# Row means of a 64 MiB tensor: other part sizes, larger load buffers, 12 loads of data in place of 14

## The chip, the core and the metric

The kernel runs on one core of one Trainium2 chip. The time is that of one execution on the device in microseconds (us): a median of 160.5 us over three runs, from 160.44 to 160.51. The profile shows one further execution of the same program, with the start and length of each instruction and of each packet of the DMA engines, which move data between the chip's main memory (HBM) and the core's own memory (SBUF).

## What is computed

```python
def setup_inputs():
    batch, seq, dim = 32, 512, 1024
    return {"x": np.random.randn(batch, seq, dim).astype(np.float32), "divisor": float(dim)}

def reference(x, divisor):
    return (np.sum(x, axis=-1) / divisor).astype(np.float32)
```

There are 32 x 512 = 16384 rows of 1024 floats, and each row becomes one number. The input is 64 MiB, read once; the output is 64 KiB. With 128 partitions each partition has J = 128 rows of 4 KiB.

## The kernel before

**Parts.** The rows are cut in three parts. The first part gives F rows to each partition, the main part M, the last part L, with F + M + L = 128 (L147 to L149). In HBM the first part is a block of its own at the front of x: partition p has rows p x F to p x F + F - 1, so that two partitions' rows lie F x 4 KiB apart (L150). Behind it each partition has W = M + L rows in one piece, the main part's first, and the distance between partitions is W x 4 KiB (L151, L152). The output has the same three parts (L153 to L155). Before, F = L = 16, M = 96, W = 112.

**Loads.** The lists `first`, `main` and `last` (L158 to L160) name the loads: a pair (rows, on_act) is one DMA that brings so many rows to every partition, and of these rows the last on_act are summed by ScalarE (ACT in the profile), the others by VectorE (DVE). All DMAs are issued by SyncE (SP) and stand in its one queue, which 16 DMA engines work off in the order of issue; `keep_in_program_order` (L182) holds that order to the order of the text. There are 12 loads into tiles `t`, and two of half a row each (`pa`, `pb`, L219 and L220) for the last row: 14 loads of data.

**Buffers.** The loads of `first` and `main`, and those of `last` with more than 4 rows, take turns in three buffers of 14 rows (pool `bulk`, L166 and L200); the loads of 4 and 2 rows have tiles of their own (`t4`, `t2`). A load into a bulk buffer waits on SP until the sums of the load three before it are done. Everything that stands behind it in SP's order waits with it.

**Sums.** In the first and main part one `reduce_sum` (L205) of VectorE sums all of a load's rows but ScalarE's; ScalarE sums a row with one ACTIVATE (L186). When a part is through, GpSimd (POOL) multiplies its sums by 1/1024 (L207). In the last part VectorE sums each row by an instruction of its own, which adds the row's two halves and scales at once (`dve_mean`, L192), and ScalarE scales as it sums. The last row comes as two halves: the sum of `pa` is put behind the elements of `pb`, and one last `dve_mean` over `pb` closes it (L226, L227).

**Stores.** The first part's means are stored by the DMA of L223, the main part's by L224, both behind all loads in SP's order, and the last part's by L228 after the last sum.

**The order by hand.** Three functions change the finished program. `start_loads_at_once` moves those loads that stand ahead of SP's first wait to the very start of the program: the first three. `latest_wait_first` sorts the waits of an instruction. `close_while_storing` lets the last store run beside the program's closing steps. The change leaves all three alone.

Of the kernel before, what the change touches and what calls it, by code (L numbers as in the profile page):

```python
# [9 lines left out]
F32 = mybir.dt.float32  # L10
# [115 lines left out]
@with_exitstack  # L126
def kernel(
    ctx: ExitStack,
    tc: tile.TileContext,
    x: bass.AP,  # L130
    divisor: float,
    out: bass.AP,
):
    nc = tc.nc
    landed = nc.alloc_semaphore("landed")
    nc.at_finalize(start_loads_at_once)
    nc.at_finalize(latest_wait_first)
    nc.at_finalize(lambda nc: close_while_storing(nc, landed))
    xf = x.flatten_outer_dims()
    N, D = xf.shape  # L140
    P = nc.NUM_PARTITIONS
    scale = 1.0 / float(divisor)
    J = N // P
    assert J * P == N


    F, L = 16, 16  # L147
    M = J - F - L
    W = M + L  # L149
    x_first = bass.AP(tensor=x.tensor, offset=0, ap=[[F * D, P], [D, F], [1, D]])  # L150
    x_main = bass.AP(tensor=x.tensor, offset=P * F * D, ap=[[W * D, P], [D, M], [1, D]])  # L151
    x_last = bass.AP(tensor=x.tensor, offset=P * F * D + M * D, ap=[[W * D, P], [D, L], [1, D]])  # L152
    o_first = bass.AP(tensor=out.tensor, offset=0, ap=[[F, P], [1, F]])  # L153
    o_main = bass.AP(tensor=out.tensor, offset=P * F, ap=[[W, P], [1, M]])
    o_last = bass.AP(tensor=out.tensor, offset=P * F + M, ap=[[W, P], [1, L]])  # L155


    first = [(2, 0), (14, 0)]  # L158
    main = [(14, 0)] * 5 + [(14, 4), (12, 5)]
    last = [(9, 4), (4, 2), (2, 1)]  # L160
    assert sum(n for n, _ in first) == F
    assert sum(n for n, _ in main) == M and sum(n for n, _ in last) == L - 1

    pad = ctx.enter_context(tc.tile_pool(name="pad", bufs=1))
    pad.tile([P, 224], F32, name="pad")
    bulk = ctx.enter_context(tc.tile_pool(name="bulk", bufs=3))  # L166
    one = ctx.enter_context(tc.tile_pool(name="one", bufs=1))
    psum = ctx.enter_context(tc.tile_pool(name="junk", bufs=4, space=bass.MemoryType.PSUM))


    c = 512
    t4 = one.tile([P, 4, D], F32, name="t4")
    t2 = one.tile([P, 2, D], F32, name="t2")
    pa = one.tile([P, 768], F32, name="pa")[:, :c]
    pb = one.tile([P, D - c + 16], F32, name="pb")[:, : D - c + 2]
    res0 = one.tile([P, F], F32, name="res0")
    res = one.tile([P, M], F32, name="res")
    fin = one.tile([P, L], F32, name="fin")
    nc.gpsimd.memset(pb[:, D - c :], 0.0)  # L179

    def load(dst, src):
        tc.keep_in_program_order(nc.sync.dma_start(out=dst, in_=src))  # L182

    def act_sum(dst, src, by=1.0):
        junk = psum.tile([P, D], F32, name="junk")
        nc.scalar.activation(junk, src, COPY, scale=by, accum_out=dst)  # L186

    def dve_mean(dst, src, by=scale):


        h = src.shape[-1] // 2
        nc.vector.tensor_tensor_reduce(  # L192
            out=src[:, :h], in0=src[:, :h], in1=src[:, h:], scale=by, scalar=0.0,
            op0=ADD, op1=ADD, accum_out=dst,
        )

    for loads, src, dst in ((first, x_first, res0), (main, x_main, res)):
        j = 0
        for rows, on_act in loads:
            t = bulk.tile([P, 14, D], F32, name="t")  # L200
            load(t[:, :rows, :], src[:, j : j + rows, :])
            d = rows - on_act
            for i in range(d, rows):
                act_sum(dst[:, j + i : j + i + 1], t[:, i, :])
            nc.vector.reduce_sum(out=dst[:, j : j + d], in_=t[:, :d, :], axis=AX)  # L205
            j += rows
        nc.gpsimd.tensor_scalar_mul(out=dst, in0=dst, scalar1=scale)  # L207
    j = 0
    for rows, on_act in last:
        t = bulk.tile([P, 14, D], F32, name="t")[:, :rows, :] if rows > 4 else t4 if rows == 4 else t2  # L210
        load(t, x_last[:, j : j + rows, :])
        d = rows - on_act
        for i in range(rows):
            if i < d:
                dve_mean(fin[:, j + i : j + i + 1], t[:, i, :])
            else:
                act_sum(fin[:, j + i : j + i + 1], t[:, i, :], by=scale)
        j += rows
    load(pa, x_last[:, j, :c])  # L219
    load(pb[:, : D - c], x_last[:, j, c:])  # L220


    tc.keep_in_program_order(nc.sync.dma_start(out=o_first, in_=res0))  # L223
    tc.keep_in_program_order(nc.sync.dma_start(out=o_main, in_=res))  # L224

    dve_mean(pb[:, D - c : D - c + 1], pa, by=1.0)  # L226
    dve_mean(fin[:, j:], pb)  # L227
    tc.keep_in_program_order(nc.sync.dma_start(out=o_last, in_=fin))  # L228
# [35 lines left out]
```

## Time and profile before

| what | value |
|---|---|
| median of 3 runs | 160.5 us (160.44 to 160.51) |
| span of the profiled execution, first to last instruction | 159.0 us |
| own time of the profiled execution, start and end included | not given; the runs' median lies 1.5 us above the span |
| VectorE busy | 117.2 us, 29 instructions |
| ScalarE busy | 18.5 us, 33 instructions |
| GpSimd busy | 1.0 us, 7 instructions |
| packets of SP's queue | 2448, 67.18 MB |
| bytes moved over the span, mean | 422 GB/s |
| VectorE idle ahead of L205, waiting for loads | 34.0 us in 9 times |
| SP waiting for L205 before it issues a load | 92.8 us in 7 times, 15.1 at most |
| SP waiting for GpSimd before the store of L224 | 21.6 us, once |

How to read it: a line of the timeline has the start in us, the length in us, the engine, the line of the program, the operation, what it writes and reads, and in square brackets how long the engine was idle before it and what ended that. A line of the groups by form has the same names, then the count, and after the bar the busy time in us, the mean length of one instruction in ns, and the idle time before. A line of the DMA issues ends with the size and the time from issue to landing, in which waiting in the queue is included. The row of GB/s has the bytes moved in each of 40 equal slices of the span, some 4 us each. The chain of work that ended last is followed backwards from the last instruction, at each step to what released it.

### The profile page before, as it was taken

How to read it: one execution, taken by the hardware profiler on the slowest of the kernel's cores; microseconds unless marked ns; L12 is line 12 of the kernel's file. 1: busy time of each engine (PE TensorE's matmuls, PEld its weight loads, DVE VectorE, ACT ScalarE, POOL GpSimd, SP SyncE). 2: the span in 40 equal slices, each digit the busy share in tenths (PEclk: the TensorE clock that was granted, in tenths of full speed). 3: DMA queues.
4: the chain of work that ended last, by engine and by line, in shares of the span. 5: the costliest groups of instructions: out<-in, count | busy, mean ns of one | idle time of the engine just before them, and what ended most of it. 6: DMA issues, size and time to landing. Idle time of an engine off the chain costs nothing.

```text
span 159.0 us, 148 instructions
## 1 busy us (share of the span) xinstructions
DVE 117.2 (74%) x29; ACT 18.5 (12%) x33; POOL 1.0 (1%) x7
## 2 busy tenths in 40 slices
DVE  0500059995999599978999599959995996395643
ACT  3000000000000000000000000000000900390684
POOL 0000000000000000000000000000000000001000
DMA  7999999959999999699999999699999999999894
GB/s 278 447 462 462 462 462 462 462 260 433 462 462 462 462 462 462 303 390 462 462 462 462 462 462 404 303 447 462 462 462 429 396 396 408 482 445 445 350 420 169
DMA packets 2448, 67.18 MB, mean 422 GB/s; under 512 B 656, under 2 KB 656, under 8 KB 912
## 3 DMA queue, kind: packets, MB, share of 16 engines
q1 hardware_dynamic: 2448, 67.18, 98.3%
HBM read 67.11 MB, written 0.07 MB: 422 GB/s over the span
## 4 chain that ended last, share of the span: by engine, by line
DMA 77%; DVE 21%; SPq 1%; issue 0%; DVEq 0%
DMA t<-in_x_dram 56%; DMA pb<-in_x_dram 21%; DVE res L205 20%; SPq L182 1%; DVE pb L192 0%; DVEq L259 0%
## 5 line engine op out<-in xcount | busy, mean ns | idle before, releaser
L205 DVE TENSOR_REDUCE res<-t 128x14 f32<-128x14336 f32 (+3 forms) x9 | 111.2, 12360 | 34.0 <-DMA t<-in_x_dram 34.0
L186 ACT ACTIVATE junk<-t 128x1024 f32<-128x1024 f32 x16 | 16.2, 1013 | 136.8 <-DMA t<-in_x_dram 136.8
L192 DVE CUSTOM_DVE_ANT_0 t<-t 128x512 f32<-128x512 f32 x8 | 5.1, 688 | 6.1 <-DMA t<-in_x_dram 6.1
L186 ACT ACTIVATION_READ_ACCUMULATOR junk<-t 128x1 f32 x16 | 3.0, 186 | 0.0
L207 POOL TENSOR_SCALAR res<-res 128x16 f32<-128x16 f32 (+1 forms) x2 | 0.7, 352 | 143.3 <-DVE res L205 143.3
L186 ACT ACT_TABLE_LOAD x1 | 1.3, 1283 | 1.7 <-PEq L245 1.7
L192 DVE DVE_READ_ACCUMULATOR2_ANT fin<- 128x1 f32 x9 | 0.7, 82 | 0.0
L192 DVE CUSTOM_DVE_ANT_0 pb<-pb 128x257 f32<-128x257 f32 x1 | 0.4, 428 | 0.2 <-DMA pb<-in_x_dram 0.2
L192 DVE CUSTOM_DVE_ANT_0 pa<-pa 128x256 f32<-128x256 f32 x1 | 0.4, 426 | 0.0
L179 POOL MEMSET pb<- 128x2 f32 x1 | 0.1, 99 | 1.3 <-POOLq L245 1.3
L245 POOL MEMSET const-bfloat16-1.0<- 128x1 bf16 x1 | 0.1, 101 | 0.0
L245 POOL MEMSET const-uint8-127<- 128x1 uint8 x1 | 0.1, 101 | 0.0
L245 POOL MEMSET const-float32-0.0<- 128x1 f32 x1 | 0.1, 98 | 0.2 <-issue 0.2
L245 POOL MEMSET const-float32-1.0<- 128x1 f32 x1 | 0.1, 98 | 0.0
L192 DVE DVE_READ_ACCUMULATOR2_ANT pb<- 128x1 f32 x1 | 0.1, 84 | 0.0
## 6 DMA issues: line engine op xcount, KB each, us to landing
t<-in_x_dram SPq DMA_DIRECT2D x7, 7168.0 KB, 35.6
t<-in_x_dram SPq DMA_DIRECT2D x1, 6144.0 KB, 33.3
t<-in_x_dram SPq DMA_DIRECT2D x1, 4608.0 KB, 27.2
t<-in_x_dram SPq DMA_DIRECT2D x2, 1024.0 KB, 19.2
t<-in_x_dram SPq DMA_DIRECT2D x1, 2048.0 KB, 31.7
pa<-in_x_dram SPq DMA_DIRECT2D x1, 256.0 KB, 33.8
pb<-in_x_dram SPq DMA_DIRECT2D x1, 256.0 KB, 33.9
out_dram<-res SPq DMA_DIRECT2D x1, 48.0 KB, 11.6
```

Source lines behind the costliest of these rows:

```text
L179: nc.gpsimd.memset(pb[:, D - c :], 0.0)
L182: tc.keep_in_program_order(nc.sync.dma_start(out=dst, in_=src))
L186: nc.scalar.activation(junk, src, COPY, scale=by, accum_out=dst)
L192: nc.vector.tensor_tensor_reduce(out=src[:, :h], in0=src[:, :h], in1=src[:, h:], scale=by, scalar=0.0, op0=ADD, op1=ADD, accum_out=dst,)
L205: nc.vector.reduce_sum(out=dst[:, j : j + d], in_=t[:, :d, :], axis=AX)
L207: nc.gpsimd.tensor_scalar_mul(out=dst, in0=dst, scalar1=scale)
L245: nc = _bacc.Bacc("TRN2", target_bir_lowering=False, num_devices=1)
```

## The change

F and L become 32, so M is 64 and W is 96. The loads become seven of 16 rows (two in the first part, four in the main part, one at the head of the last part), then 8, 5 and 2 rows and the two half rows: 12 loads of data. The three bulk buffers grow to 16 rows, the tile `t4` goes, and the 5-row load takes a bulk buffer. ScalarE has no rows in the main part any more; in the last part it has 5 of 16, 3 of 8, 2 of 5 and 1 of 2. One partition's run in a load of 16 rows is 64 KiB, where 14 rows were 56 KiB. Three loads, the first of them of 16 rows in place of 2, still stand ahead of SP's first wait.

```diff
-    F, L = 16, 16
+    F, L = 32, 32
...
-    first = [(2, 0), (14, 0)]
-    main = [(14, 0)] * 5 + [(14, 4), (12, 5)]
-    last = [(9, 4), (4, 2), (2, 1)]
+    first = [(16, 0)] * 2
+    main = [(16, 0)] * 4
+    last = [(16, 5), (8, 3), (5, 2), (2, 1)]
...
-    t4 = one.tile([P, 4, D], F32, name="t4")
...
-            t = bulk.tile([P, 14, D], F32, name="t")
+            t = bulk.tile([P, 16, D], F32, name="t")
...
-        t = bulk.tile([P, 14, D], F32, name="t")[:, :rows, :] if rows > 4 else t4 if rows == 4 else t2
+        t = bulk.tile([P, 16, D], F32, name="t")[:, :rows, :] if rows > 2 else t2
```

## The prediction

> **What bounds the kernel now.** I read the page's head first, then the chain of work that ended last, then the timeline of VectorE's reductions, and last the queue's table and the waits.
>
> ```profile
> span 159.0 us, 148 instructions
> DVE 117.2 (74%) x29; ACT 18.5 (12%) x33; POOL 1.0 (1%) x7
> ...
> DMA 77%; DVE 21%; SPq 1%; issue 0%; DVEq 0%
> ...
> q1 hardware_dynamic: 2448, 67.18, 98.3%
> ```
>
> No engine is busy for more than 74% of the span, while the packets of SP's one queue fill 98.3% of the 16 DMA engines' time. That queue is the bound. The chain gives 20% to the reductions of L205, and that share is misleading: it is followed through the semaphore that lets a load be issued, though such a load then stands in the queue behind other loads for tens of us. Whether those loads were ever late shows in the landings. The timeline prints them, because each of these instructions starts 0.02 us after its load has landed:
>
> ```profile
> 4.63 2.29 DVE L205 TENSOR_REDUCE res<-t 128x2 f32<-128x2048 f32 x1 [4.63 <-DMA t<-in_x_dram]
> 21.51 15.09 DVE L205 TENSOR_REDUCE res<-t 128x14 f32<-128x14336 f32 x1 [14.59 <-DMA t<-in_x_dram]
> 38.44 15.09 DVE L205 TENSOR_REDUCE res<-t 128x14 f32<-128x14336 f32 x1 [1.84 <-DMA t<-in_x_dram]
> ...
> 123.10 10.82 DVE L205 TENSOR_REDUCE res<-t 128x10 f32<-128x10240 f32 x1 [1.88 <-DMA t<-in_x_dram]
> 137.65 7.62 DVE L205 TENSOR_REDUCE res<-t 128x7 f32<-128x7168 f32 x1 [3.73 <-DMA t<-in_x_dram]
> 148.49 0.69 DVE L192 CUSTOM_DVE_ANT_0 t<-t 128x512 f32<-128x512 f32 x1 [3.22 <-DMA t<-in_x_dram]
> 153.37 0.69 DVE L192 CUSTOM_DVE_ANT_0 t<-t 128x512 f32<-128x512 f32 x1 [1.73 <-DMA t<-in_x_dram]
> 155.86 0.69 DVE L192 CUSTOM_DVE_ANT_0 t<-t 128x512 f32<-128x512 f32 x1 [1.17 <-DMA t<-in_x_dram]
> 157.10 0.43 DVE L192 CUSTOM_DVE_ANT_0 pb<-pb 128x257 f32<-128x257 f32 x1 [0.17 <-DMA pb<-in_x_dram]
> ```
>
> From 21.51 to 123.10 six loads of 14 rows land, 16.93 us apart. Then 12 rows take 14.55 us, 9 rows 10.84, 4 rows 4.88 and 2 rows 2.49. Put through the ends (2 rows 2.49, 14 rows 16.93), a straight line gives **1.203 us a row and 0.083 us a load**. It returns 14.52, 10.91 and 4.90 for the other three, within 0.07. The landings are evenly paced, so nothing that SP or VectorE does leaves the DMA engines without work. The row of slices seems to say otherwise:
>
> ```profile
> GB/s 278 447 462 462 462 462 462 462 260 433 462 462 462 462 462 462 303 390 462 462 462 462 462 462 404 303 447 462 462 462 429 396 396 408 482 445 445 350 420 169
> ```
>
> The dips to 260 and 303 look like starvation, yet the landings on both sides of 36 us are 16.93 us apart like all others. Seen in quarters of a us, the bytes stand in lumps 2.1 us apart and nothing between: a packet is booked in one moment, 16 engines in step, and a slice of 4 us holds two lumps or one. The dips are grain, not lost time, and a change that cures them cures nothing. At 7168 KB in 16.93 us the pace is 433.6 GB/s throughout.
>
> **The change, part by part.** The sum is made against the profiled execution (span 159.0 us); 1.5 us lie around the span, as the median of the runs is 160.5, and I carry those over unchanged.
>
> *Fewer loads.* There are 128 rows per partition before and after, so 128 x 1.203 = 154.0 us of transfer stay. With the two half rows there are 14 loads before and 12 after: 2 x 0.083 = **0.17 us less**. The Trainium skill ("DMA: Bandwidth & Descriptors", section "Anatomy of one DMA") fits about 2.0 us of fixed cost for a DMA on GpSimd's path; applied to two dropped loads it would make 4 us of gain and 156.5 us. The trace speaks against it here: the 2-row load lands 2.49 us after the one ahead of it, of which 2.41 us are rows, because queued loads overlap that cost.
>
> *The first load of 16 rows instead of 2.* The 2-row load lands at 4.61; less 2.49 that is 2.12 us that no row explains. Windows of a quarter us show the first bytes at 1.0, and bytes reach full pace by 2.25. What one large run per partition does there the trace cannot show. The ramp is paid once, at best disappears and at worst doubles, so I bound it by its whole length beyond the time its bytes need: about 0.6 us either way. I take 0, since the latency in front of the first byte doesn't depend on what follows. VectorE starts at about 21.5 instead of 4.6, which costs nothing: its reductions have to wait for loads either way, as below.
>
> *Three buffers of 16 rows.* The new landings, from 2.12 + 19.33 a load of 16 rows: 21.5, 40.8, 60.1, 79.5, 98.8, 118.1, 137.4; then 8 rows 147.2, 5 rows 153.3, 2 rows 155.8 and the half rows to 156.9. VectorE's duration comes from the rows by form:
>
> ```profile
> L205 DVE TENSOR_REDUCE res<-t 128x14 f32<-128x14336 f32 x6 | 90.5, 15086 | 23.8 <-DMA t<-in_x_dram 23.8
> ...
> L205 DVE TENSOR_REDUCE res<-t 128x2 f32<-128x2048 f32 x1 | 2.3, 2286 | 4.6 <-DMA t<-in_x_dram 4.6
> ```
>
> (15.086 - 2.286) / 12 = 1.067 us a row, so 16 rows take 15.09 + 2 x 1.067 = 17.22 us, 2.1 us less than the 19.33 to the next landing. Reductions end at 38.7, 58.0, 77.4, 96.7, 116.0 and 135.3, and each end releases a buffer to the load three further on. The load released at 38.7 is needed when the third one is through, at about 60: 21 us of cover, and the same for the next four. The thinnest cover is that of the 5-row load, which takes the last bulk buffer at 135.3 and is needed at 147.2: 11.9 us. Behind it on SP stand the 2-row load, both half rows and two stores. They used to be issued from 122.1 on; at 0.33 to 0.46 us an issue they are now all out by 137.7, and the first of them is needed at 153. So the later issue costs 0; if that cover were gone, the end would move us for us.
>
> *Fewer rows on ScalarE, more on L192.* In the main part ScalarE's 9 rows disappear; VectorE now has 96 rows in reductions (6 x 17.22 = 103.3 us) and 20 with L192 at a step of 0.61 us in the timeline, 116 us in all against 117.2. The 16-row load of the last part, landing at 137.4, gives VectorE 11 rows (6.7 us, to 144.2) and ScalarE 5 rows at 1.04 (to 142.7), before 147.2. The 8 rows need 3.1 us on each, the 5 rows 1.8 and 2.3, against steps of 9.7, 6.1 and 2.5 us. The last three landings keep their order and their work (1 + 1 rows, then the half rows), so the last 0.43 us stays.
>
> *The stores.*
>
> ```profile
> out_dram<-res SPq DMA_DIRECT2D x1, 48.0 KB, 11.6
> out_dram<-res SPq DMA_DIRECT2D x1, 8.0 KB, 33.6
> out_dram<-fin SPq DMA_DIRECT2D x1, 8.0 KB, 1.4
> ```
>
> They become 32, 16 and 16 KB. The first two stand behind the loads: 8 KB issued at 123.62 lands at 157.2, 48 KB issued at 145.82 at 157.4, 0.2 us later. The main result's store no longer waits 21.6 us for GpSimd (its reduction ends at 135.3, GpSimd needs 0.4), but it only stands longer in the queue. The last store has 8 KB more: by the 0.2 us of 48 KB at most **0.03 us more**.
>
> *Where the rows lie in memory.* The distance between two partitions' rows goes from 64 to 128 KB in the first part and from 448 to 384 KB in the other; a partition's run in one load goes from 56 to 64 KB. The trace has two rows on distance: the 14-row load at 64 KB lands 16.88 us after the one ahead of it, those at 448 KB 16.93. The difference of 0.05, over 128 / 14 loads, is 0.46 us; I keep plus and minus 0.46 as bounds and take 0, as the rows nearly agree over a factor of 7 and both new distances lie between them. A rule speaks against the change: the Trainium skill (same page, section "Latency and other measured facts") reports copies that lose rate as the pitch between partitions reaches a power of two, 207 GB/s at 512 KB against 214 padded. Were that 3% to hold at 128 and 384 KB, 154 us would become 159 and the kernel 165; no run here shows such a loss.
>
> **Sum:** 159.0 - 0.17 + 0.03 = 158.9 of span, **160.4 us** with the 1.5 around it: 0.1% less. A measurement of this kernel can tell about 0.2% (0.32 us) from no change, so this is no change.
>
> **The rivals.** *Slower by memory layout.* All partitions' rows now lie at multiples of 128 KB, and 16 engines in step read them. For it: the two distances in the trace differ by 0.05 us a load. Against: the pace is the same for 2 to 14 rows, so a limit other than the order of addresses sets it. At 0.46 us it makes 160.8. It decides from 0.004 us a row (0.3%) on, and nothing hides it, as the queue is full. *Slower by splitting:* the change does not do what it says if a run of 64 KB is moved in two pieces. A load has 8 packets per engine (0.083 / 8 = 0.01 us each); seven loads of 16 rows would have 56 more, +0.6 us, 161.0. The count of packets would show it. *Slower by late issue:* the 5-row load misses its place, from 11.9 us of delay on; the landings would have to be a whole load off. At 2 us beyond, it makes 162.4. *Faster at the start:* long runs swallow the ramp, -0.6 us, 159.8. For it: full pace comes only at 2.25 us. Against: latency ahead of the first byte isn't shortened by longer runs.
>
> **How the numbers follow.** Forecast 0.76; memory layout 0.09, splitting 0.05, late issue 0.02, together 0.16 slower; faster start 0.08. The range runs from 160.0 to 160.9: the sum with half of the ramp's bound downward, and the 0.46 of the layout upward; it leaves out the late issue, most of the faster start and of the splitting, and a layout loss of per cents.
>
> **What would show it.** Right: loads of 16 rows 19.3 us apart, the reductions each with about 2 us idle ahead of them, the pb row's load at about 156.9, the first reduction at about 21.5, 2160 packets (288 fewer: two loads of 128 and their 16 closing ones each). Wrong: a load that lands late after an idle queue, a step over 19.4 us, a first landing outside 20.9 to 22.1, or some 900 packets more.

## The result and the profile after

The changed kernel takes 161.03 us (five executions, 160.80 to 161.35) where the kernel before takes 160.50 (160.44 to 160.57): a ratio of 1.0036, 95% interval 1.0024 to 1.0048. It is 0.5 us slower, where no change was forecast, and lies outside the range of 160.0 to 160.9.

The head of its page and the queue's line:

```profile
span 159.7 us, 155 instructions
DVE 116.7 (73%) x50; ACT 13.2 (8%) x23; POOL 1.0 (1%) x7
...
q1 hardware_dynamic: 2160, 67.18, 97.9%
```

The same engines are as busy as forecast (VectorE 116.7 us, forecast 116), and the packets are the 2160 that were forecast, so a run of 64 KB is not split. The queue is still what bounds the kernel. The profiled execution is the slowest of the five (161.35; the spans of the five are 159.2, 159.3, 159.4, 159.7 and 159.7). From its timeline, the lines that begin with a landing:

```profile
21.75 17.22 DVE L204 TENSOR_REDUCE res<-t 128x16 f32<-128x16384 f32 x1 [21.75 <-DMA t<-in_x_dram]
41.05 17.22 DVE L204 TENSOR_REDUCE res<-t 128x16 f32<-128x16384 f32 x1 [2.08 <-DMA t<-in_x_dram]
60.38 17.22 DVE L204 TENSOR_REDUCE res<-t 128x16 f32<-128x16384 f32 x1 [2.12 <-DMA t<-in_x_dram]
...
118.39 17.22 DVE L204 TENSOR_REDUCE res<-t 128x16 f32<-128x16384 f32 x1 [2.06 <-DMA t<-in_x_dram]
137.73 0.69 DVE L191 CUSTOM_DVE_ANT_0 t<-t 128x512 f32<-128x512 f32 x1 [2.12 <-DMA t<-in_x_dram]
147.50 0.69 DVE L191 CUSTOM_DVE_ANT_0 t<-t 128x512 f32<-128x512 f32 x1 [2.95 <-DMA t<-in_x_dram]
153.89 0.69 DVE L191 CUSTOM_DVE_ANT_0 t<-t 128x512 f32<-128x512 f32 x1 [3.23 <-DMA t<-in_x_dram]
156.47 0.69 DVE L191 CUSTOM_DVE_ANT_0 t<-t 128x512 f32<-128x512 f32 x1 [0.66 <-DMA t<-in_x_dram]
157.80 0.43 DVE L191 CUSTOM_DVE_ANT_0 pb<-pb 128x257 f32<-128x257 f32 x1 [0.26 <-DMA pb<-in_x_dram]
```

The middle is as worked out: loads 19.33 us apart (forecast 19.33), reductions of 17.22 us, some 2.1 us of idle time ahead of each, and no load of 16 rows late. Two places differ. The first landing is at 21.73, 0.28 later than the 21.45 of the forecast's formula (2.12 + 19.33), and that lateness stays to the end. And the 5-row load lands 6.39 us after the 8-row load, where 6.10 were forecast; with the next steps that makes another 0.5 us.

A third place is outside the span. The times and spans of the same executions differ by 1.60 to 1.69 us here. For the kernel before, on the chips of the later runs, the difference is 1.28 to 1.38, with a median of 1.33. What the trace has there is one packet of q14, a queue that it calls "instruction" and that I take to bring the engines' code; the window from 159.7 to 162 us of the changed kernel:

```profile
DMA packets 1, 0.01 MB, mean 4 GB/s; under 512 B 0, under 2 KB 0, under 8 KB 0
## 3 DMA queue, kind: packets, MB, share of 16 engines
q14 instruction: 1, 0.01, 1.0%
```

The trace of before has no packet at all in its window from 159 to 162 us.

So there were three suspects: **the head** (a first load of 16 rows), **the tail** (late small loads, by the layout, by the 11 pairs of VectorE instructions that sum the seventh load, or by chance), and **what lies around the span** (the code). The experiments take them apart.

### The profile page after: what moved, and what is told of

It reads as the page before. It is cut to its first block, busy times and chain, and to the rows that moved or that the text cites. A ratio compares the mean times of both kernels' runs of the same rounds, so it can differ in the third digit from the quotient of the medians.

```text
span 159.7 us, 155 instructions
## 1 busy us (share of the span) xinstructions
DVE 116.7 (73%) x50; ACT 13.2 (8%) x23; POOL 1.0 (1%) x7
## 2 busy tenths in 40 slices
DMA packets 2160, 67.18 MB, mean 421 GB/s; under 512 B 624, under 2 KB 624, under 8 KB 880
## 3 DMA queue, kind: packets, MB, share of 16 engines
q1 hardware_dynamic: 2160, 67.18, 97.9%
## 4 chain that ended last, share of the span: by engine, by line
DMA 64%; DVE 33%; another core or an unknown queue 1%; SPq 1%; issue 0%; DVEq 0%
DMA t<-in_x_dram 51%; DVE res L204 32%; DMA pb<-in_x_dram 13%; SPq L181 1%; DVE pb L191 0%; DVEq L258 0%
## 5 line engine op out<-in xcount | busy, mean ns | idle before, releaser
L204 DVE TENSOR_REDUCE res<-t 128x16 f32<-128x16384 f32 x6 | 103.3, 17219 | 32.3 <-DMA t<-in_x_dram 32.3
L185 ACT ACTIVATE junk<-t 128x1024 f32<-128x1024 f32 x11 | 11.2, 1014 | 142.7 <-DMA t<-in_x_dram 142.7
L191 DVE CUSTOM_DVE_ANT_0 t<-t 128x512 f32<-128x512 f32 x20 | 12.6, 690 | 9.0 <-DMA t<-in_x_dram 9.0
L185 ACT ACTIVATION_READ_ACCUMULATOR junk<-t 128x1 f32 x11 | 2.1, 187 | 0.0
L191 DVE DVE_READ_ACCUMULATOR2_ANT fin<- 128x1 f32 x21 | 1.8, 84 | 0.0
L206 POOL TENSOR_SCALAR res<-res 128x32 f32<-128x32 f32 (+1 forms) x2 | 0.7, 332 | 133.6 <-DVE res L204 133.6
```

Source lines behind the costliest of these rows:

```text
L191: nc.vector.tensor_tensor_reduce(out=src[:, :h], in0=src[:, :h], in1=src[:, h:], scale=by, scalar=0.0, op0=ADD, op1=ADD, accum_out=dst,)
```

## The experiments

All edits are to the changed kernel unless the text says otherwise. "Around" is the median of time minus span over a kernel's executions. "Pairs" says whether VectorE's 11 rows of the seventh load of 16 rows are summed by 11 pairs of instructions, as in the changed kernel, or by one reduction. Each kernel is compared with executions of the kernel before on the same chip.

| label | rows of the first load | KiB between partitions: first part, others | pairs | median us | median span | around | ratio to before (95%) |
|---|---|---|---|---|---|---|---|
| again | 16 | 128, 384 | yes | 161.03 | 159.40 | 1.63 | 1.0033 (1.0021 to 1.0045) |
| head2 | 2 | 128, 384 | yes | 160.67 | 159.35 | 1.33 | 1.0013 (1.0005 to 1.0022) |
| pitch | 16 | 64, 448 | no | 160.73 | 159.40 | 1.34 | 1.0015 (1.0006 to 1.0023) |
| reduce6 | 16 | 128, 384 | no | 160.69 | 159.35 | 1.36 | 1.0019 (1.0009 to 1.0030) |
| before2 | 2 | 64, 448 | | 160.46 | 159.10 | 1.32 | 1.0001 (0.9992 to 1.0010) |
| pad1 | 16 | 128, 384 | yes | 160.74 | 159.40 | 1.36 | 1.0020 (1.0010 to 1.0030) |
| both | 2 | 64, 448 | no | 160.52 | 159.20 | 1.32 | 1.0000 (0.9991 to 1.0009) |
| head14 | 14 | 64, 448 | | 160.64 | 159.30 | 1.34 | 1.0010 (1.0001 to 1.0018) |
| head2r | 2 | 128, 384 | no | 160.54 | 159.20 | 1.33 | 1.0000 (0.9991 to 1.0008) |
| pairs | 2 | 64, 448 | yes | 160.52 | 159.20 | 1.33 | 1.0003 (0.9995 to 1.0012) |
| lay14 | 2 | 128, 384 | | 160.97 | 159.30 | 1.64 | 1.0033 (1.0021 to 1.0044) |
| head1 | 1 | 64, 448 | no | 161.01 | 159.70 | 1.32 | 1.0034 (1.0022 to 1.0046) |
| pad1_b | 16 | 128, 384 | yes | 160.73 | 159.40 | 1.35 | 1.0007 (0.9996 to 1.0019) |
| pairs16 | 16 | 64, 448 | yes | 160.81 | 159.50 | 1.34 | 1.0011 (1.0001 to 1.0021) |
| head2_b | 2 | 128, 384 | yes | 160.56 | 159.20 | 1.32 | 0.9996 (0.9985 to 1.0007) |
| head2r_b | 2 | 128, 384 | no | 160.63 | 159.30 | 1.34 | 0.9998 (0.9987 to 1.0010) |
| head4 | 4 | 64, 448 | no | 160.53 | 159.20 | 1.35 | 1.0007 (0.9998 to 1.0015) |
| head8 | 8 | 64, 448 | no | 160.56 | 159.20 | 1.35 | 1.0007 (0.9998 to 1.0016) |

The kernels before2, head14 and lay14 have the 14-row loads of the kernel before. The medians of the kernel before in the five groups of runs (again to reduce6, before2 to head14, head2r to head1, pad1_b to head2r_b, the last two) are 160.49, 160.50, 160.49, 160.53 and 160.46.

### The changed kernel again, and three variants

**again** has no edit.

> The changed kernel itself, to see what of its +0.5 us stands in every execution and what comes and goes. Its five runs lay between 160.80 and 161.35 us, the profiled one being the slowest. Two pieces stand out in that profile: the first landing at 21.73 instead of the predicted 21.5 (about +0.25), and a 5-row load that landed 6.38 us after the 8-row load where 6.10 were predicted, with another 0.2 us lost to the end (about +0.5 in all). Theory A (the head costs in every run, the tail only in some): first landing again at 21.7, the tail between 0 and +0.5, time 160.8 to 161.3, median 161.0. Rival (the tail's loss is fixed by the layout and the load sizes): the 5-row load again lands 6.4 us after the 8-row load, time 161.3. If the whole difference is a matter of the chip: 160.4.

The same median to a hundredth, 160.85 to 161.30, spans from 159.2 to 159.7, and 1.59 to 1.69 around. So some 1.6 us around the span are in every execution, while the 0.5 us between the spans of 159.2 and 159.7 come and go. In its profile the first landing is at 21.71, and the 5-row load is late again (6.28 us).

**head2** gives the first part a head of 2 rows.

```diff
-    first = [(16, 0)] * 2
+    first = [(2, 0), (14, 0), (16, 0)]
```

> The changed kernel with a head of 2 and 14 rows in place of the first 16 (three loads in the first part, the first two as in the kernel before, one load more in all). Theory A1 (a first load of long runs costs about 0.25 us of ramp, which the whole queue carries to the end): first landing at 4.6, the second reduction at about 21.5, and 0.25 less 0.08 for the extra load, 160.85 against 161.0 for the changed kernel. Rival A2 (the 128 KiB distance between partitions costs the ramp): the first landing comes at 4.85 and the time is 161.1. The third load now takes a new buffer order, which costs nothing as SP issues it at once. The tail is untouched, so its 0 to 0.5 us stays.

160.67, but for another reason than theory A1 has: 1.33 us around in place of 1.63, and a median span of 159.35, hardly shorter. This first landing was at 4.90, near the 4.85 of rival A2; but the kernel both, below, has 4.86 with rows 64 KiB apart, which takes A2 back.

**pitch** goes back to the old distances.

```diff
-    F, L = 32, 32
+    F, L = 16, 16
...
-    first = [(16, 0)] * 2
-    main = [(16, 0)] * 4
-    last = [(16, 5), (8, 3), (5, 2), (2, 1)]
+    first = [(16, 0)]
+    main = [(16, 0)] * 5 + [(16, 5)]
+    last = [(8, 3), (5, 2), (2, 1)]
```

> The changed kernel's load sizes and buffers with the distances between partitions of the kernel before (64 and 448 KiB): one load of 16 rows in the first part, six in the main part, then 8, 5, 2 rows and the two half rows. The seventh load is now summed by one reduction of 11 rows (11.9 us) beside 5 rows of ScalarE, before the 8 rows land. Theory B1 (the tail's loss comes from rows 384 KiB apart): the 5-row load lands 6.1 us after the 8-row load, the runs agree within 0.15 us, time 160.5 to 160.7 with the head's 0.25 still there, first landing 21.7. Rival B2 (it comes from the sizes and order of the small loads): 161.0 and runs as scattered as those of the changed kernel. If rows 128 KiB apart cost the head: first landing at 21.45 and 160.4.

160.73 with 1.34 around. The span's 159.40 is that of the changed kernel, so the layout does not explain it. The 5-row load is on time (6.05 us), but the first landing was at 22.01.

**reduce6** keeps the distances and sums the seventh load by one reduction.

```diff
-    F, L = 32, 32
+    F, L = 32, 16
...
-    main = [(16, 0)] * 4
-    last = [(16, 5), (8, 3), (5, 2), (2, 1)]
+    main = [(16, 0)] * 4 + [(16, 5)]
+    last = [(8, 3), (5, 2), (2, 1)]
```

> The changed kernel with its distances between partitions and all loads as they are; only the seventh load counts to the main part (L = 16, M = 80) and is summed by one reduction of 11 rows in place of 11 pairs of instructions. VectorE has 28 instructions where the changed kernel has 50, and the means of the main part are stored some 13 us later, still behind all loads. Theory B3 (22 more VectorE instructions and their writes beside the last loads slow the tail): the 5-row load lands 6.1 us after the 8-row load, time 160.5 to 160.7, and what lies around the span goes from 1.6 back to 1.5 us. Rivals B1 and B2 (layout or load sizes): 161.0, scattered from 160.8 to 161.3 like the changed kernel.

160.69, around 1.36, span 159.35. Its executions run from 160.55 to 161.31, so the scatter stays without the pairs. Its loads and distances are those of the changed kernel, and still only 1.36 us lie around the span. That points away from the loads and to the engines' programs; the next run changes VectorE's alone.

### One VectorE instruction more

```diff
     nc.gpsimd.memset(pb[:, D - c :], 0.0)
+    nc.vector.memset(fin[:, :1], 0.0)
```

> The changed kernel with one more VectorE instruction, a memset of one element per partition at the start, which lies beside nothing. The changed kernel's executions all have 1.60 to 1.69 us around the span, where the kernel before and the three variants have 1.29 to 1.38; its trace shows one packet of the instruction queue 1.1 us after the span's end. Theory C (the end of VectorE's program lies just behind a border of the code that is fetched ahead, and the program's end waits for that fetch): one instruction more shifts the border, as in the variant with the head of 2 rows, and 1.33 us lie around the span: 160.7 in place of 161.0. Rival (the 0.3 us come from the 12 loads, the first of 16 rows, or the stores of this kernel): 1.6 us around the span and 161.0.

The instruction adds work and takes time away: around falls from 1.63 to 1.36 and the median from 161.03 to 160.74, while the span's median stays at 159.40. So these **0.3 us** come neither from the loads nor from the stores, which are the same in both; where VectorE's program ends decides them, as theory C forecast. The code packet is still there in the same window, at a different place (slices of 0.0575 us; for the changed kernel, it stands in the 20th, here in the 14th; first pad1, then the changed kernel):

```profile
GB/s 0 0 0 0 0 0 0 0 0 0 0 0 0 142 0 0 0 0 0 0 0 0 0 0 0 0 0 0 0 0 0 0 0 0 0 0 0 0 0 0
```

```profile
GB/s 0 0 0 0 0 0 0 0 0 0 0 0 0 0 0 0 0 0 0 142 0 0 0 0 0 0 0 0 0 0 0 0 0 0 0 0 0 0 0 0
```

That is 160.5 and 160.8 us: the packet comes 0.9 and 1.1 us after the ends of the spans (159.6 and 159.7). With its waits counted, VectorE's program has 61 instructions in the trace of the changed kernel and 62 in pad1's. The other kernels agree: head2, pairs, pairs16, pad1_b and head2_b have 62, a code packet at the end, and 1.32 to 1.35 us around; those without pairs have 38 to 40, no such packet, and 1.32 to 1.36. Only one other kernel has 61, lay14 below, and it has 1.64, though its program was written for another purpose. Hence neither the packet as such (62 instructions have it too) nor the length as such (62 are more) costs, but an end at one certain place. With 61 the packet comes 1.1 to 1.3 us after the end of the span (the changed kernel, again, lay14), with 62 at 0.5 to 0.9. That the closing code then has to wait for it would fit, but the trace shows no instruction there, nor for which engine the packet is; this part is argued. The Trainium skill ("Runtime: NRT & Kernel Launch", section "Instruction fetch mechanics") says that an engine fetches the next block of its code by itself while it executes, and that crossing a block's border is mostly hidden. If the packet is such a block, these runs agree for 62 instructions and not for 61.

### The head

**before2** is the kernel before.

> The kernel before, run against itself, for a profile of it on the chip of these runs and as a measure of how far two equal kernels stand apart here. Expected: 160.5 us, ratio 1.000 within 0.001, span 159.1 to 159.2 and 1.33 us around it, first landing (2 rows) at 4.6, all engines' packets of one size alike. If the head of 2 rows also lands at 4.9, as it did with rows 128 KiB apart, then the first landing scatters by 0.3 us between executions whatever the kernel.

160.46 and a ratio of 1.0001 (0.9992 to 1.0010). The first landing was at 4.76 in place of 4.61, the 16 rows at 21.64 in place of 21.49: first landings move by 0.15 us between executions of one kernel.

**both** has the large buffers with the parts and the head of the kernel before.

```diff
-    F, L = 32, 32
+    F, L = 16, 16
...
-    first = [(16, 0)] * 2
-    main = [(16, 0)] * 4
-    last = [(16, 5), (8, 3), (5, 2), (2, 1)]
+    first = [(2, 0), (14, 0)]
+    main = [(16, 0)] * 5 + [(16, 5)]
+    last = [(8, 3), (5, 2), (2, 1)]
```

> The large buffers and loads of 16 rows from the third load on, with the parts and the head of the kernel before: 2 and 14 rows 64 KiB apart, then six loads of 16 rows, 8, 5, 2 rows and the half rows 448 KiB apart. 13 loads in place of 14. Theory A (a head of 16 rows is what costs the span 0.2 us, the layout with 384 KiB only makes executions scatter): span 159.0 to 159.2, 1.33 around it, 160.4 us, scatter as small as that of the kernel before. Rival (64 KiB runs or 16-row buffers cost by themselves): 160.7 as with the other two variants.

160.52 (160.38 to 160.60), as the kernel before. Against pitch it differs in the head alone: 160.73 to 160.52, **0.2 us for a head of 16 rows**, in which one load less is contained. (They ran on two chips, where the kernel before has 160.49 and 160.50.) The 64 KB runs and the buffers cost nothing that is seen, and 13 loads in place of 14 gain nothing that is seen.

Where the 0.2 us lie shows in two lines of each profile, the one that follows the landing of the sixteenth row and the one that follows the last half row (first pitch, then both):

```profile
22.03 17.22 DVE L204 TENSOR_REDUCE res<-t 128x16 f32<-128x16384 f32 x1 [22.03 <-DMA t<-in_x_dram]
...
157.55 0.43 DVE L191 CUSTOM_DVE_ANT_0 pb<-pb 128x257 f32<-128x257 f32 x1 [0.27 <-DMA pb<-in_x_dram]
```

```profile
21.76 15.09 DVE L204 TENSOR_REDUCE res<-t 128x14 f32<-128x14336 f32 x1 [14.59 <-DMA t<-in_x_dram]
...
157.33 0.43 DVE L191 CUSTOM_DVE_ANT_0 pb<-pb 128x257 f32<-128x257 f32 x1 [0.21 <-DMA pb<-in_x_dram]
```

From one to the other it takes 135.52 and 135.57 us. The other profiles without late loads agree: in reduce6, pad1_b and pairs16 (head of 16 rows) 135.52 to 135.59, in head2r, pairs and head2_b (2 rows) 135.54 to 135.62. So the head's cost is all there before the sixteenth row is in. Single landings of the sixteenth row scatter about as much as that cost: 21.73 to 22.01 in the four with a head of 16 rows, 21.62 to 21.74 in the four with 2. Hence the medians decide its size.

**head14** exchanges the first two loads of the kernel before.

```diff
-    first = [(2, 0), (14, 0)]
+    first = [(14, 0), (2, 0)]
```

> The kernel before with the first two loads exchanged: 14 rows first, then 2. All sizes, distances, sums and stores stay. The load that waits for the first buffer is issued at about 34 and needed at about 38, so nothing starves. Theory A1 (a first load with long runs costs about 0.2 us of ramp): the second load's end, 16 rows in all, comes at about 21.75 in place of 21.5 and the time is 160.7. Rival (the head costs nothing, the span's 0.2 us come from elsewhere): 160.5.

160.64, ratio 1.0010 (1.0001 to 1.0018). The same rows with the long run first cost 0.14 us. The 16 rows were in at 21.79.

**head1** (from both) goes the other way.

```diff
-    first = [(2, 0), (14, 0)]
+    first = [(1, 0), (15, 0)]
```

> The variant with large buffers, rows 64 and 448 KiB apart and a head of one row in place of two, then 15 rows: 13 loads as before. Theory A1 (the ramp grows with the run of the first load): at most a further 0.02, since from 2 to 14 rows it grew by 0.15: 160.5, no gain. If the ramp is set by the first packet's length in another way, a head half as long gives back up to 0.15: 160.35, which would beat the kernel before.

Neither theory: 161.01, the span longer by 0.5. The first row lands at 4.02, and the line below it has 22.21 for 16 rows, where both has 21.76 (first head1, then both):

```profile
4.05 1.22 DVE L204 TENSOR_REDUCE res<-t 128x1 f32<-128x1024 f32 x1 [4.05 <-DMA t<-in_x_dram]
22.21 16.15 DVE L204 TENSOR_REDUCE res<-t 128x15 f32<-128x15360 f32 x1 [16.95 <-DMA t<-in_x_dram]
```

```profile
4.88 2.29 DVE L204 TENSOR_REDUCE res<-t 128x2 f32<-128x2048 f32 x1 [4.88 <-DMA t<-in_x_dram]
21.76 15.09 DVE L204 TENSOR_REDUCE res<-t 128x14 f32<-128x14336 f32 x1 [14.59 <-DMA t<-in_x_dram]
```

**head4** and **head8** (from both) fill the gap with `first = [(4, 0), (12, 0)]` and `first = [(8, 0), (8, 0)]`.

> Large buffers, rows 64 and 448 KiB apart, a head of 4 rows, then 12. If the cost grows with the length of the first run from 2 rows on: 160.55 (0.02 above the variant with 2 rows). If the ramp has its best point at somewhat longer runs: 160.4, below the kernel before. If 2 rows are a lucky point: 160.7.

> The same with a head of 8 rows, then 8. If the cost grows with the length of the first run: 160.6, half way to the 160.73 of a head of 16. If every head but 2 rows costs the same: 160.7.

160.53 and 160.56, with median spans of 159.20, as with 2 rows. Against the kernel before on the same chip, heads of 2, 4, 8, 14 and 16 rows stand at +0.02, +0.07, +0.10, +0.14 and +0.24 us (both, head4, head8, head14, pitch), each give or take some 0.15, and a head of one row at +0.52. So one row is worst, 2 to 8 rows are best, and 14 and 16 cost 0.1 to 0.2 us more; whether the cost is flat up to 8 rows or grows slowly with the length, these runs don't tell. No head beats the kernel before. Why the start behaves so stays open.

### Layout, pairs, or chance in the tail

**head2r** is head2 with the sums of reduce6.

```diff
-    F, L = 32, 32
+    F, L = 32, 16
...
-    first = [(16, 0)] * 2
-    main = [(16, 0)] * 4
-    last = [(16, 5), (8, 3), (5, 2), (2, 1)]
+    first = [(2, 0), (14, 0), (16, 0)]
+    main = [(16, 0)] * 4 + [(16, 5)]
+    last = [(8, 3), (5, 2), (2, 1)]
```

> The layout by itself, at the load sizes of the variant with large buffers and the head of 2 rows (160.52 us): the same 13 loads and sums, with F = 32, L = 16, so that rows lie 128 and 384 KiB apart in place of 64 and 448. Theory B1 (this layout makes packets late now and then, some 0.2 us in the median, with executions scattered over 0.5 us): 160.7, runs from 160.45 to 161.1. Rival (the 11 pairs of VectorE instructions made the difference between the two variants with a head of 2 rows): 160.5, runs within 0.2 us.

160.54, from 160.43 to 160.65: against both (160.52) the layout costs nothing that is seen. Theory B1 (the layout) falls.

**pairs** is both with the seventh 16-row load counted to the last part.

```diff
-    F, L = 32, 32
+    F, L = 16, 32
...
-    first = [(16, 0)] * 2
-    main = [(16, 0)] * 4
+    first = [(2, 0), (14, 0)]
+    main = [(16, 0)] * 5
```

> The variant with large buffers and the head of 2 rows, with the seventh load of 16 rows counted to the last part (F = 16, L = 32, rows still 64 and 448 KiB apart): its 11 rows are summed by 11 pairs of VectorE instructions in place of one reduction. Theory B1 (layout): 160.5 and small scatter, as without the pairs. Theory B3 (the pairs slow the tail): 160.7 with a 5-row load that lands later than 6.1 us after the 8-row load. Theory C adds nothing here if VectorE's program ends off the border: it has one instruction more than the changed kernel, so 1.33 us around the span; 1.6 would speak for the length of the program as such.

160.52 with the 5-row load on time: the pairs alone cost nothing that is seen either.

**lay14** has the new parts with the buffers and the load sizes of the kernel before (the diff is to that kernel).

```diff
-    F, L = 16, 16
+    F, L = 32, 32
...
-    first = [(2, 0), (14, 0)]
-    main = [(14, 0)] * 5 + [(14, 4), (12, 5)]
-    last = [(9, 4), (4, 2), (2, 1)]
+    first = [(2, 0), (14, 0), (14, 0), (2, 0)]
+    main = [(14, 0)] * 3 + [(14, 4), (8, 3)]
+    last = [(14, 5), (11, 4), (4, 2), (2, 1)]
```

> The new parts alone: the kernel before with its buffers of 14 rows and its head of 2 rows, but F = L = 32, so that rows lie 128 and 384 KiB apart; loads of 2, 14, 14, 2, then 14, 14, 14, 14, 8, then 14, 11, 4, 2 and the half rows, 15 in all. One load more costs 0.08. Theory B1 (the layout makes packets late whatever their size): 160.8 with a wide scatter. Rival (only 64 KiB runs in this layout do): 160.55 to 160.6 with the scatter of the kernel before.

160.97 looks like B1's 160.8 and is not: 1.64 us around, with a span of 159.30, 0.15 above the kernel before's on that chip with one load more. It is the kernel with 61 VectorE instructions named above, met by chance.

Since head2 had scattered on one chip and head2r had not on another, four kernels were put on one chip. **pad1_b**, **head2_b** and **head2r_b** repeat their namesakes; **pairs16** is pad1 in the old layout.

```diff
-    F, L = 32, 32
+    F, L = 16, 32
...
-    first = [(16, 0)] * 2
-    main = [(16, 0)] * 4
+    first = [(16, 0)]
+    main = [(16, 0)] * 5
...
     nc.gpsimd.memset(pb[:, D - c :], 0.0)
+    nc.vector.memset(fin[:, :1], 0.0)
```

> The changed kernel with one VectorE instruction more, on the chip of the next three. Layout or pairs or both at work: 160.75 with runs from 160.55 to 161.2, 5-row load more than 6.2 us after the 8-row load. If the chip of its first run did it: 160.65 with runs within 0.2 us and 6.05.

> The same with F = 16 (rows 64 and 448 KiB apart), one load moved from the first to the main part: head of 16 rows, 11 pairs of VectorE instructions and the longer program stay. Theory B1 (layout): 160.65 to 160.7 (the head's cost stays), runs within 0.25 us, 5-row load 6.05 us after the 8-row load. Theory B3 (pairs): like the run before it, late and scattered.

> The changed kernel with a head of 2 and 14 rows, 128 and 384 KiB, with pairs. On its first chip 160.67, from 160.41 to 161.03. If layout and pairs act together whatever the chip: 160.65 and that scatter again, against 160.54 in the next. If it was the chip: 160.54 and runs within 0.25 us.

> The same layout and head without the pairs, L = 16. 160.54 and runs within 0.25 us if the pairs or the chip made the difference; 160.65 and scatter if the layout alone did and its first chip was a quiet one.

With a head of 16 rows 160.73 and 160.81, with 2 rows 160.56 and 160.63: the head again, and neither layout (160.73 to 160.81 has the wrong sign) nor pairs (160.56 to 160.63, too). On this chip the kernel before itself ran from 160.38 to 161.28. What an execution with a long time looks like, head2r_b's profile shows, taken from its slowest one (161.11):

```profile
40.96 17.22 DVE L204 TENSOR_REDUCE res<-t 128x16 f32<-128x16384 f32 x1 [4.29 <-DMA t<-in_x_dram]
60.59 17.22 DVE L204 TENSOR_REDUCE res<-t 128x16 f32<-128x16384 f32 x1 [2.41 <-DMA t<-in_x_dram]
80.03 17.22 DVE L204 TENSOR_REDUCE res<-t 128x16 f32<-128x16384 f32 x1 [2.22 <-DMA t<-in_x_dram]
99.60 17.22 DVE L204 TENSOR_REDUCE res<-t 128x16 f32<-128x16384 f32 x1 [2.36 <-DMA t<-in_x_dram]
```

The steps are 19.63, 19.44 and 19.57 us in place of 19.3, here in the middle, while the 5-row load is on time. Loads come late in stretches of some executions, and the kernel before has executions just as long. In the profiles of the changed kernel, again and pad1, all from executions slower than the median, it was the 5-row load each time (6.3 to 6.4 us after the 8-row load); in pad1_b, the same program as pad1, it was on time (6.0). Whether three times the same load is chance stays open, and these runs name no cause.

## Why the prediction was wrong, point by point

**What bounds the kernel: right.** The queue is full in both kernels, and landings are even.

**Carrying over the 1.5 us around the span: this step failed.** The sentence "I carry those over unchanged" hid a term of **+0.30 us** (1.63 against 1.33), more than all other terms of the sum. Nothing in the profile of before shows it, since VectorE's program has 38 instructions there, waits counted, and no code packet follows it; but the change adds 21 VectorE instructions to the 29 that the page counts, and no term was set for that. In its place the runs showed a cost of the place where that program ends: one instruction more took it away (pad1), and of all kernels only those with 61 have it. The 1.5 itself was 1.33 around the span and some 0.2 by which the profiled execution was shorter than the median one (159.0 against 159.2).

**The first load of 16 rows: mis-sized.** Taken as 0 with bounds of 0.6 us either way; measured +0.14 (14 rows) to +0.2 (16 rows). It was inside its bounds, and of the sign opposite to that of the rival of a faster start, which is refuted. The reason for 0, that the time ahead of the first byte is the same, did hold (the first packet starts at 1.00 to 1.03 us in every trace); what is lost is lost behind it.

**Fewer loads: not confirmed.** 0.083 us a load came out of a line through landings. One load less gave 160.52, 160.54 and 160.52 (both, head2r, pairs) against 160.49 to 160.50: nothing, or 0.03 us more. The 0.083 us are below what these medians resolve (about 0.15). The profiles speak against it: between the two lines shown for pitch and both, the same 112 rows take 135.59 and 135.55 us in 12 loads (before, before2) and 135.52 to 135.62 in 11.

**Buffers, late issue, ScalarE's rows, stores: right.** The idle times ahead of the reductions are about 2.1 us, no load is late for having waited for its buffer, and the last store lands 1.4 us after its issue, as before.

**Layout: right to take 0.** head2r and both differ by 0.02 us, pad1_b and pairs16 by -0.08. The loss that the Trainium skill ("DMA: Bandwidth & Descriptors", section "Latency and other measured facts") reports for a pitch of 512 KiB, and that would have made 165 us here, does not show at 128 and 384 KiB. **Splitting: refuted** by 2160 packets.

**The sum:** 0.3 around the span and 0.2 in it (median spans 159.4 and 159.2) make the 0.5 us that were measured. The range failed because its upper end held the layout's 0.46 but no term for the program's end; with 0.3 and the head's 0.2 added the forecast of 160.4 becomes 160.9, and without the 0.17 for fewer loads 161.0 to 161.1. (Its lower end, the sum less half of the ramp's 0.6, is nearer to 160.1 than to 160.0.)

## What to carry to other kernels

In this kernel the queue is full from end to end, and resizing its loads and buffers moved only its two ends: in such a case look at the first landing and at what follows the last one. Check time minus span for each kernel by itself before explaining a change of tenths of a us by the work in the span; here one instruction more on an engine removed such a difference. And a profile of the slowest execution shows what befell that execution along with the change: compare the spans of several executions before a late load is given a cause.

## What the runs showed of the hardware

The end of VectorE's program at a certain instruction (61 in the trace, with its waits; two programs, three runs) costs 0.3 us behind the span, one instruction later (62, six runs) nothing. A first load with a run of 4 KiB per partition costs the start 0.5 us, runs of 8 to 32 KiB at most 0.1 us, 56 and 64 KiB 0.14 to 0.24 us. Runs of 64 KiB move as one packet each, at the pace of those of 56 KiB: 19.33 us for 16 rows, 1.208 us a row, against 1.209.
